# A trunk step on one core: which engine makes the low parts of the weights around the pooling groups, and three orders beside it

## The chip, the cores and the metric

The kernel runs on one core of one Trainium2 chip (trn2). The metric is the device time of one execution in microseconds. A core has TensorE (PE in the profile; its weight loads are PEld), VectorE (DVE), ScalarE (ACT), GpSimd (POOL) and SyncE (SP), which work side by side and wait for each other by semaphores, and 16 DMA engines that carry the transfers which SP, ACT and GpSimd issue.

## The reference

One layer of a hybrid trunk over 288 columns: 256 positions of a new sequence and 8 x 4 new tokens of running ones (with 30 old convolution inputs and 15 old pooling inputs each). Cut to what matters:

```python
h = rmsnorm(x, norm1_g)
proj = h @ w_in + b_in                     # 2048 -> 3072: a | gate | z, 1024 each
u = a * sigmoid(gate)
c = silu(layernorm(depthwise_causal_conv(u, 31 taps, conv_b), ln_g, ln_b))
d = mean of z over the last w positions - z          # four groups of 256 columns, w = 2, 4, 8, 16
p = d @ pool_w[g] * pool_scale                       # 256 x 256 for each group
x = x + concat([c, p]) @ w_out                       # 2048 -> 2048
f = relu(rmsnorm(x, norm2_g) @ w_ff1) ** 2           # 2048 -> 8192
x = x + f @ w_ff2                                    # 8192 -> 2048
y = rmsnorm(x, norm_f)
```

It also returns the last 30 columns of u and the last 15 of z.

## The kernel before

**Products in parts.** Each float32 operand is held as a high part, rounded to the matmul's format (`F32R`), and a low part, the rest. For a 128x128 block of weights and 288 columns there are three matmuls: high weight by high column, low weight by high column, high weight by low column. `gemm` writes them for two blocks k, k+1 as six in a row: the two of `whi`, the two of `wlo`, then `whi` again by the columns' low parts.

**The weights' way in.** The weights come as 512 KB tiles `wr` (128 partitions, four blocks of k, 256 columns, six buffers) by loads that SP issues in the order of use. ACT copies each into its high part `whi` (L260). The low part `wlo` is made in one of three ways, by a letter of the table `WAYS`, which names a few letters for each stage of the program and repeats them (`split_part`): G, two GpSimd subtractions of 128x512 (L268); V, one DVE subtraction of 128x1024 (L265); D, ACT writes minus the high part (L262) and a DMA on GpSimd's queue adds the weights from HBM onto it (L263), called an adding transfer here. `whi` and `wlo` have five buffers each, so ACT starts on a tile when PE is done with the tile five before.

I number the weight tiles in the order of use; PE has 24 matmuls on each of 512 KB. The stages are those of `SEQUENCE`: c0 and c1 (tiles 1 to 8), c2 (9 to 12), c3 (13 to 16), c4 (17 to 20), p3 (21 to 24), c5 (25 to 28), p2 (29 to 32), P3 (33, a half tile), c6 (34 to 37), p1 (38 to 41), P2 (42), p0 (43 to 46), P1 (47), c7 (48 to 51), P0 (52). A c is the projection of one 128-column piece of a and its gate, a p that of the 256 columns of z of a pooling group, a P the product of a group with its `pool_w`. Then come the lower half of w_out, by the pool columns `mixp` (stage names w0 to w7; buffers `dx` in the trace), its upper half by the convolution's columns `mixc` (`mx` in the trace), and the MLP.

**Beside the projections.** After a c, `conv_pair` makes u (DVE L432, L436, ACT's sigmoid), and then 30 taps by DVE on the 256 columns (L448), and for the tokens one GpSimd multiplication of all 31 windows into `prd` (L451) that DVE sums (L453). The taps stand under `later()`, so DVE takes them when nothing else of it is ready. `sum_c` is the running sum of the conv columns, by GpSimd (L456). After a p, `pool_group` adds neighbours on GpSimd, w doubling (L479), corrects the first columns (L483), and forms d: DVE the 256 columns (L484), GpSimd the 32 newest (a scaling L486, in place, and a subtraction L487). ACT and DVE split d (L489, L490).

**What sets the order.** A scheduler orders each engine's instructions by the priority of where they are written, with `later()` as an offset and `tc.issue_after` as a tie. Within some gemms the table `TURN` reorders the first 48 matmuls by a pattern of classes. PSUM banks (`ac`) have two pairs; a product starts when DVE has emptied the pair (L470, L432, in w_out the addition to x, L579).

The change touches `load`, `split_part`, `gemm`, `weight_groups`, `conv_pair`, `pool_group` and the lines of the main function that call them.

Of the kernel before, what the change touches and what calls it, by code (L numbers as in the profile page):

```python
# [86 lines left out]
def trunk_kernel(ctx: ExitStack, tc: tile.TileContext, io):  # L87
# [163 lines left out]

    turns = {}

    def split_part(raw, src, hi, lo, way):

        nc.scalar.copy(hi, raw)  # L260
        if way == "D":
            nc.scalar.activation(lo, f32(hi), AF.Copy, scale=-1.0)  # L262
            nc.gpsimd.dma_start(lo, src, accum_op=ALU.add)  # L263
        elif way == "V":
            nc.vector.tensor_tensor(lo, raw, f32(hi), op=ALU.subtract)  # L265
        else:
            for j in range(0, raw.shape[1], 2):
                nc.gpsimd.tensor_tensor(lo[:, j : j + 2, :], raw[:, j : j + 2, :], f32(hi[:, j : j + 2, :]), op=ALU.subtract)  # L268

# [25 lines left out]

    def gemm(banks, rhs, m_outer=False, between={}, classes="", by_part=False, gets=None, pairs=None):

# [129 lines left out]
    def conv_pair(i, banks):  # L427
# [9 lines left out]
        if i % 2 == 0:  # L437
            cs.append(actp.tile([P, 2, T], F32, name=nm("c"), tag="c", bufs=4))
        c = cs[i // 2][:, i % 2, :]
        with later():  # L440
# [10 lines left out]
            nc.gpsimd.tensor_tensor(prd[:, :, :, 0:CW], windows(us, CW), cwv[:, None, None, :].to_broadcast([P, NB, NS, CW]), op=ALU.mult)  # L451
# [12 lines left out]
    def pool_group(g):  # L464
# [19 lines left out]
        nc.vector.scalar_tensor_tensor(out=d[:, :, 0:SEQ], in0=s[:, :, PH:ZO], scalar=1.0 / w, in1=z[:, :, PH:ZO], op0=ALU.mult, op1=ALU.subtract)  # L484
# [1 line left out]
        nc.gpsimd.tensor_scalar(news[0], news[0], 1.0 / w, None, op0=ALU.mult)  # L486
        nc.gpsimd.tensor_tensor(d[:, :, SEQ:T].rearrange("p m (b t) -> p m b t", t=NS), news[0], news[1], op=ALU.subtract)  # L487
        dh, dl = act2("dx", tag="p", bufs=4)
# [50 lines left out]
    gemm(each(bks[0]) + each(bks[1]), proj, gets=[lambda k, m: both_gets[m // 2][0](k, m % 2)], between={(0, 2): lambda: pool_products(0)}, classes="." * 36 + TURN, pairs=early + [(6, m) for m in range(4)])  # L539
    chain.clear()  # L540
# [241 lines left out]
```

## Time and profile before

| | |
|---|---|
| median of 3 runs | 1081.81 us (1081.7 to 1082.16) |
| the profiled execution's own time | 1082.43 us |
| its span, first to last instruction | 1080.6 us |
| granted TensorE clock, mean | 0.998 |
| PE busy | 1069.2 us, 99% of the span, 8176 matmuls |
| DVE, ACT, POOL busy | 633.7, 479.0, 175.9 us |
| adding transfers (L263) | 7 of 512 KB |

Times are in microseconds from the span's start. A timeline row gives a start, a length, the engine, the line, and what it writes and reads; neighbours of one kind are put together (x6), and brackets hold the idle time ahead and what ended it. A row of the chain of waits gives a start, a length and a count of instructions that follow one another on the path that ended last. A row of stretches gives, for a window, its length and each engine's busy time with its count, then the granted clock, the DMA engines' mean busy share and what they moved in GB/s.

### The profile page before, as it was taken

The page shows a single profiled execution, that of the slowest core. Times are in us where ns is not written, and L with a number is a line of the kernel's source. Part 1 is how long each engine was busy: PE and PEld are TensorE (multiplying, and loading weights), DVE is VectorE, ACT ScalarE, POOL GpSimd, SP SyncE. Part 2 cuts the span into 40 slices and gives each one's busy share as a digit, 9 for nine tenths or more (in the row PEclk, how much of TensorE's full clock was granted, in tenths as well). Part 3 has the DMA queues.
Part 4 walks back from the last instruction along what each step waited for, and adds up shares of the span by engine and source line. Part 5 has one row for each costly group of instructions (what it writes and reads, how often), then busy time and mean ns, then how long its engine had stood idle before and what let it go on. Part 6 is the DMA issues. An engine that isn't in the chain of part 4 may idle for free.

```text
span 1080.6 us, 19528 instructions
## 1 busy us (share of the span) xinstructions
PE 1069.2 (99%) x8176; PEld 1067.9 (99%) x8176; DVE 633.7 (59%) x810; ACT 479.0 (44%) x588; POOL 175.9 (16%) x182
## 2 busy tenths in 40 slices
PE   9999999999999999999999999999999999999996
PEld 8999999999999999999999999999999999999996
DVE  7899999788654544444554444555544445554553
ACT  8654445665544433334443333444433334444441
POOL 0878979512000000000000000000000000000001
PEclk9999999999999999999999999999999999999999
DMA  9896478555555555555555555555555555555522
GB/s 326 288 263 182 145 187 247 177 171 173 162 173 166 169 175 163 170 173 165 170 174 164 170 170 167 171 173 162 173 168 167 173 171 164 173 166 170 172 79 88
DMA packets 58296, 190.71 MB, mean 176 GB/s; under 512 B 6240, under 2 KB 11232, under 8 KB 58208
## 3 DMA queue, kind: packets, MB, share of 16 engines
q1 hardware_dynamic: 56336, 184.35, 54.3%
q0 software_dynamic: 1008, 3.67, 1.9%
q8 instruction: 64, 1.05, 0.4%
q10 hardware_dynamic: 864, 1.44, 0.4%
q14 instruction: 24, 0.20, 0.0%
HBM read 185.16 MB, written 4.28 MB: 175 GB/s over the span
## 4 chain that ended last, share of the span: by engine, by line
PE 75%; issue 21%; ACT 2%; POOL 1%; DMA 1%; SPq 0%; POOLq 0%; DVE 0%
PE ac L291 74%; POOL wlo L268 1%; DMA wr<-in_w 1%; ACT whi L349 1%; PE pp L291 1%; DMA wlo<-in_w 1%; ACT hx L354 0%; ACT z_all L405 0%; POOL prd L451 0%; POOL xT L718 0%; ACT whi L260 0%; SPq L191 0%; POOLq L768 0%; DVE xT L691 0%; ACT whi L356 0%
## 5 line engine op out<-in xcount | busy, mean ns | idle before, releaser
L260 ACT CAST whi<-wr 128x1024 fp32r<-128x1024 f32 (+1 forms) x332 | 346.5, 1044 | 551.3 <-PE ac L291 536.7
L265 DVE TENSOR_TENSOR wlo<-wr,whi 128x1024 fp32r<-128x1024 f32 x288 | 353.5, 1227 | 348.1 <-ACT whi L260 348.1
L291 PE MATMUL ac<-ax,whi 128*128 128x288 f32 x2048 | 351.0, 292 | 0.0
L291 PE MATMUL ac<-fx,whi 128*128 128x288 f32 x2048 | 350.2, 292 | 0.0
L291 PEld LDWEIGHTS ac<-ax,whi 128*128 128x128 f32 x2048 | 296.0, 187 | 0.0
L291 PEld LDWEIGHTS ac<-fx,whi 128*128 128x128 f32 x2048 | 295.6, 187 | 0.0
L291 PE MATMUL ac<-ax,wlo 128*128 128x288 f32 x1024 | 217.3, 292 | 0.0
L291 PE MATMUL ac<-fx,wlo 128*128 128x288 f32 x1024 | 216.4, 292 | 0.0
L291 PEld LDWEIGHTS ac<-ax,wlo 128*128 128x128 f32 x1024 | 162.5, 187 | 0.0
L291 PEld LDWEIGHTS ac<-fx,wlo 128*128 128x128 f32 x1024 | 162.2, 187 | 0.0
L291 PE MATMUL ac<-hx,whi 128*128 128x288 f32 x768 | 131.9, 296 | 1.4 <-DVE hx L352 1.4
L718 POOL TENSOR_TENSOR xT<-xT,rf 128x288 f32<-128x288 f32 x4 | 3.1, 795 | 799.9 <-ACT rf L722 799.9
L291 PEld LDWEIGHTS ac<-hx,whi 128*128 128x128 f32 x768 | 112.6, 190 | 1.8 <-ACT hx L354 1.7
L268 POOL TENSOR_TENSOR wlo<-wr,whi 128x512 fp32r<-128x512 f32 x74 | 102.4, 1433 | 17.1 <-ACT whi L260 16.0
L448 DVE SCALAR_TENSOR_TENSOR pc<-u_all,vec,pc 128x256 f32<-128x256 f32 x232 | 99.3, 479 | 1.9 <-ACT pc L445 0.7
L291 PE MATMUL ac<-hx,wlo 128*128 128x288 f32 x384 | 80.4, 295 | 0.2 <-DMA wlo<-in_w 0.2
L291 PEld LDWEIGHTS ac<-hx,wlo 128*128 128x128 f32 x384 | 61.1, 189 | 0.4 <-DMA wlo<-in_w 0.4
L291 PE MATMUL ac<-dx,whi 128*128 128x288 f32 x256 | 46.8, 295 | 0.0
L291 PE MATMUL ac<-mx,whi 128*128 128x288 f32 x256 | 44.9, 293 | 0.0
L660 DVE SCALAR_TENSOR_TENSOR t<-ac,r 128x576 f32<-128x576 f32 x32 | 24.2, 757 | 25.4 <-PE ac L291 25.3
L291 PEld LDWEIGHTS ac<-dx,whi 128*128 128x128 f32 x256 | 38.4, 188 | 0.2
L291 PEld LDWEIGHTS ac<-mx,whi 128*128 128x128 f32 x256 | 37.5, 188 | 0.2 <-DVE xT L579 0.2
(129 smaller groups left out, 529.6 us busy)
## 6 DMA issues: line engine op xcount, KB each, us to landing
wr<-in_w SPq DMA_DIRECT2D x335, 512.0 KB, 3.8
wlo<-in_w POOLq DMA_DIRECT2D x7, 512.0 KB, 7.8
xT<-in_xT SPq DMA_DIRECT2D x8, 288.0 KB, 7.7
wr<-in_w SPq DMA_DIRECT2D x5, 256.0 KB, 3.9
out_u_out<-u_all SPq DMA_DIRECT2D x1, 1208.0 KB, 9.6
u_all<-in_hist_c SPq DMA_DIRECT2D x8, 136.0 KB, 5.3
out_z_out<-z_all SPq DMA_DIRECT2D x1, 668.0 KB, 9.2
z_all<-in_hist_p SPq DMA_DIRECT2D x4, 152.0 KB, 6.6
```

The costliest lines, as they stand in the source:

```text
L260: nc.scalar.copy(hi, raw)
L265: nc.vector.tensor_tensor(lo, raw, f32(hi), op=ALU.subtract)
L268: nc.gpsimd.tensor_tensor(lo[:, j : j + 2, :], raw[:, j : j + 2, :], f32(hi[:, j : j + 2, :]), op=ALU.subtract)
L291: last = nc.tensor.matmul(*args, **kw)
L349: nc.scalar.copy(hi[:, blocks[0]], raw[:, blocks[0]])
L448: nc.vector.scalar_tensor_tensor(out=dst, in0=up[:, w : w + SEQ], scalar=cwv[:, w : w + 1], in1=pc, op0=ALU.mult, op1=ALU.add)
L660: nc.vector.scalar_tensor_tensor(out=t, in0=bk[:, :, :T], scalar=0.0, in1=both(rows2[0]), op0=ALU.max, op1=ALU.mult)
L718: eng.tensor_tensor(xk, xk, r[:, None, :].to_broadcast([P, n, T]), op=ALU.mult)
```

## The change

It does six things.

1. `WAYS`: c4 turns from GDGD to GGGD (tile 18: G for D), p3 keeps GDDG under the general letter p, p2 turns from GVVG to GDDG (tiles 30 and 31: D for V), p1 to GVDG (tile 40), p0 to GDVG (tile 44), and w0 from VV to GV. Four low parts of pooling groups go from DVE to adding transfers, one of c4 goes from a transfer to GpSimd, and one of w0 from DVE to GpSimd: ten transfers for seven.
2. The multiplication `prd` is tied behind an adding transfer (first ones) or behind the newest columns of a pooling group (i over 4), and the taps of c2 and c3 are written one stage later.
3. `pool_group` writes GpSimd's part of d (scaling and newest columns) ahead of DVE's part.
4. GpSimd's subtractions of later tiles are tied behind a group's newest columns (`pooled`).
5. The halves of the tiles w0 to w7 are loaded and used in exchanged order (`load((1, 0))`, `^ 4`), the first 24 matmuls of the first w_out product put the columns' high parts ahead of the low parts, and the pool products P1 and P0 begin earlier inside the products around them.
6. In the first product over `mixc` the pairs of k and column block are taken in another order (`mixed`).

```diff
-WAYS = {... "c4": "GDGD", "p3": "GDDG", "c5": "GDGD", "c": "GGGV", "p": "GVVG", "w0": "VV", ...}
+WAYS = {... "c4": "GGGD", "c5": "GDGD", "c": "GGGV", "p0": "GDVG", "p1": "GVDG", "p": "GDDG", "w0": "GV", ...}
-    def load():
+    def load(order=(0, 1)):
-        for h in range(2):
+        for h in order:
-    turns = {}
+    turns, added, newest, pooled = {}, [], {}, []
         if way == "D":
             nc.scalar.activation(lo, f32(hi), AF.Copy, scale=-1.0)
-            nc.gpsimd.dma_start(lo, src, accum_op=ALU.add)
+            added.append(nc.gpsimd.dma_start(lo, src, accum_op=ALU.add))
...
-                nc.gpsimd.tensor_tensor(lo[:, j : j + 2, :], raw[:, j : j + 2, :], ...)
+                with tc.issue_after(pooled[-1].ins) if pooled else nullcontext():
+                    nc.gpsimd.tensor_tensor(lo[:, j : j + 2, :], raw[:, j : j + 2, :], ...)
...
+        todo[:late] = sorted(todo[:late], key=lambda p: p[2])          # in gemm, late=0 by default
...
-            get = split(load(), f"w{j}")
-            yield [lambda k, m, get=get: get(korder[k], m)]
+            get = split(load((1, 0)), f"w{j}")
+            yield [lambda k, m, get=get: get(korder[k] ^ 4, m)]
...
+        while waiting:                                                  # in conv_pair
+            taps(*waiting.pop())
+        if i in (2, 3):
+            waiting.append((i, up, us))
+        else:
+            taps(i, up, us)
+    def taps(i, up, us):
...
-            nc.gpsimd.tensor_tensor(prd[:, :, :, 0:CW], windows(us, CW), ...)
+            with tc.issue_after((newest[{5: 3, 6: 2, 7: 0}[i]] if i > 4 else added[max(0, min(2, i - 1))]).ins):
+                nc.gpsimd.tensor_tensor(prd[:, :, :, 0:CW], windows(us, CW), ...)
...
-        nc.vector.scalar_tensor_tensor(out=d[:, :, 0:SEQ], in0=s[:, :, PH:ZO], ...)
         news = [...]
         nc.gpsimd.tensor_scalar(news[0], news[0], 1.0 / w, None, op0=ALU.mult)
-        nc.gpsimd.tensor_tensor(d[:, :, SEQ:T]..., news[0], news[1], op=ALU.subtract)
+        last = nc.gpsimd.tensor_tensor(d[:, :, SEQ:T]..., news[0], news[1], op=ALU.subtract)
+        newest[g] = last
+        nc.vector.scalar_tensor_tensor(out=d[:, :, 0:SEQ], in0=s[:, :, PH:ZO], ...)
...
+        if i == 7:
+            pooled.append(newest[1])
-   ... between={12: lambda: pool_products(1)}
+   ... between={8: lambda: pool_products(1)}
         else:
+            pooled.append(newest[i])
             pool_products(i)
+    pooled.append(newest[0])
...
+    mixed = [(k, m) for k in range(0, KT // 2, 2) for m in range(4)]
+    mixed.sort(key=lambda km: (km[0] // 4, km[1] // 2) if km[0] < 4 else (1, 0))
-    gemm(... between={(0, 2): lambda: pool_products(0)}, classes="." * 36 + TURN, pairs=early + [(6, m) for m in range(4)])
+    gemm(... late=24, between={4: lambda: pool_products(0)}, classes="." * 24 + TURN, pairs=early + [(6, m) for m in range(4)])
...
-    gemm(each(bks[0]) + each(bks[1]), mixc, gets=[...])
+    gemm(each(bks[0]) + each(bks[1]), mixc, gets=[...], pairs=mixed)
```

The scheduler's result on GpSimd at the start of c3: the low part of tile 13 (`wlo_604`), the adding transfer of tile 14 (`wlo_609`), the multiplications of c0 and c1 and the low part of tile 15 (`wlo_618`). Before:

```order
L268 TENSOR_TENSOR wlo_604<-wr_599,whi_603 128x512 x2
L451 TENSOR_TENSOR prd_667<-u_all,vec 128x32x31
L451 TENSOR_TENSOR prd_708<-u_all,vec 128x32x31
L263 DMA wlo_609<-in_w 128x1024
L268 TENSOR_TENSOR wlo_618<-wr_613,whi_617 128x512 x2
```

and now:

```order
L269 TENSOR_TENSOR wlo_604<-wr_599,whi_603 128x512 x2
L263 DMA wlo_609<-in_w 128x1024
L463 TENSOR_TENSOR prd_667<-u_all,vec 128x32x31
L463 TENSOR_TENSOR prd_708<-u_all,vec 128x32x31
L269 TENSOR_TENSOR wlo_618<-wr_613,whi_617 128x512 x2
```

The transfer is issued ahead of the two multiplications. GpSimd again, from the sums of p1 to p0: the low part of tile 41 (`wlo_1703` before, `wlo_1706` now), that of tile 43 (`wlo_1894`, `wlo_1897`), tile 46 (`wlo_1911`, `wlo_1915`), and now the transfers of tile 40 (`wlo_1701`) and tile 44 (`wlo_1902`). Before:

```order
L479 TENSOR_TENSOR s_1528<-s_1525 128x416 x2
L268 TENSOR_TENSOR wlo_1703<-wr_1696,whi_1702 128x512 x2
L483 TENSOR_TENSOR s_1528<-s_1528,rcnt 128x2x7
L486 TENSOR_SCALAR s_1528<-s_1528 128x2x8x4
L487 TENSOR_TENSOR d_1531<-s_1528,z_all 128x2x32
L451 TENSOR_TENSOR prd_1746<-u_all,vec 128x32x31
L268 TENSOR_TENSOR wlo_1894<-wr_1889,whi_1893 128x512 x2
L268 TENSOR_TENSOR wlo_1911<-wr_1904,whi_1910 128x512 x2
```

and now:

```order
L263 DMA wlo_1701<-in_w 128x1024
L491 TENSOR_TENSOR s_1530<-s_1527 128x416 x2
L269 TENSOR_TENSOR wlo_1706<-wr_1698,whi_1705 128x512 x2
L495 TENSOR_TENSOR s_1530<-s_1530,rcnt 128x2x7
L497 TENSOR_SCALAR s_1530<-s_1530 128x2x8x4
L498 TENSOR_TENSOR d_1533<-s_1530,z_all 128x2x32
L463 TENSOR_TENSOR prd_1749<-u_all,vec 128x32x31
L269 TENSOR_TENSOR wlo_1897<-wr_1892,whi_1896 128x512 x2
L468 TENSOR_TENSOR sum_c<-sum_c,c_1019 128x288
L263 DMA wlo_1902<-in_w 128x1024
L269 TENSOR_TENSOR wlo_1915<-wr_1908,whi_1914 128x512 x2
```

The two transfers stand among the sums, and the transfer of tile 44 stands behind the subtraction of tile 43 and an addition to `sum_c`. PE at the start of the products over `mixc`: `ac22` is the pair of banks of column blocks 0 and 1, `ac23` that of 2 and 3. Before:

```order
728 L291 MATMUL ac22_2841<-mx1_2816,whi69_2741 128x288 x4
729 L291 MATMUL ac22_2841<-mx1_2816,wlo69_2742 128x288 x2
730 L291 MATMUL ac22_2841<-mx1_2816,whi69_2741 128x288 x2
731 L291 MATMUL ac23_2842<-mx1_2816,whi71_2803 128x288 x2
732 L291 MATMUL ac23_2842<-mx1_2816,wlo71_2804 128x288 x2
733 L291 MATMUL ac23_2842<-mx1_2816,whi71_2803 128x288 x4
```

and now:

```order
722 L292 MATMUL ac22_2846<-mx1_2821,whi69_2746 128x288 x4
723 L292 MATMUL ac22_2846<-mx1_2821,wlo69_2747 128x288 x2
724 L292 MATMUL ac22_2846<-mx1_2821,whi69_2746 128x288 x2
725 L292 MATMUL ac22_2846<-mx2_2828,whi69_2746 128x288 x2
726 L292 MATMUL ac22_2846<-mx2_2828,wlo69_2747 128x288 x2
727 L292 MATMUL ac22_2846<-mx2_2828,whi69_2746 128x288 x4
728 L292 MATMUL ac22_2846<-mx2_2828,wlo69_2747 128x288 x2
729 L292 MATMUL ac22_2846<-mx2_2828,whi69_2746 128x288 x2
730 L292 MATMUL ac23_2847<-mx1_2821,whi71_2808 128x288 x2
```

The first pair of banks gets 24 matmuls ahead of the second, where it got 12: its two blocks of the second columns (`mx2`) stand in between.

More of the change, by code (lines that the diff above doesn't have):

```diff
@@ L70 @@
 TURN = "110100" * 4 + "01" * 6 + "1100" * 3
-WAYS = {"c2": "GVGV", "c3": "GDGG", "c4": "GDGD", "p3": "GDDG", "c5": "GDGD", "c": "GGGV", "p": "GVVG", "w0": "VV", "w": "GG", "ff": "VV"}
+WAYS = {"c2": "GVGV", "c3": "GDGG", "c4": "GGGD", "c5": "GDGD", "c": "GGGV", "p0": "GDVG", "p1": "GVDG", "p": "GDDG", "w0": "GV", "w": "GG", "ff": "VV"}
 VEC = (("norm1_g", 16), ("b_in", 24), ("conv_b", 8), ("ln_g", 8), ("ln_b", 8), ("pool_scale", 8), ("norm2_g", 16), ("norm_f", 16))
@@ L267, in split_part @@
             for j in range(0, raw.shape[1], 2):
-                nc.gpsimd.tensor_tensor(lo[:, j : j + 2, :], raw[:, j : j + 2, :], f32(hi[:, j : j + 2, :]), op=ALU.subtract)
+                with tc.issue_after(pooled[-1].ins) if pooled else nullcontext():
+                    nc.gpsimd.tensor_tensor(lo[:, j : j + 2, :], raw[:, j : j + 2, :], f32(hi[:, j : j + 2, :]), op=ALU.subtract)
     def spl():
@@ L294, in mm, with gemm @@
         return last
-    def gemm(banks, rhs, m_outer=False, between={}, classes="", by_part=False, gets=None, pairs=None):
+    def gemm(banks, rhs, m_outer=False, between={}, classes="", by_part=False, gets=None, pairs=None, late=0):
         n = len(rhs)
@@ L412, in trunk_kernel @@
     rb = row("rb")
-    cs, pcs = [], []
+    cs, pcs, waiting = [], [], []
     sum_c = tmpp.tile([P, 2, T], F32, name="sum_c", tag="ag2", bufs=2)
@@ L450, in conv_pair @@
             nc.scalar.activation(prd[:, :, :, CW], ones[:, 0 : NB * NS].rearrange("p (b t) -> p b t", t=NS), AF.Identity, bias=v("conv_b", i), scale=0.0)
-            nc.gpsimd.tensor_tensor(prd[:, :, :, 0:CW], windows(us, CW), cwv[:, None, None, :].to_broadcast([P, NB, NS, CW]), op=ALU.mult)
+            with tc.issue_after((newest[{5: 3, 6: 2, 7: 0}[i]] if i > 4 else added[max(0, min(2, i - 1))]).ins):
+                nc.gpsimd.tensor_tensor(prd[:, :, :, 0:CW], windows(us, CW), cwv[:, None, None, :].to_broadcast([P, NB, NS, CW]), op=ALU.mult)
             cso = c[:, SEQ:T]
@@ L483, in pool_group @@
         nc.gpsimd.tensor_tensor(first_sums, first_sums, rcnt[:, None, w - 2 : 2 * w - 3].to_broadcast([P, 2, w - 1]), op=ALU.mult)
-        nc.vector.scalar_tensor_tensor(out=d[:, :, 0:SEQ], in0=s[:, :, PH:ZO], scalar=1.0 / w, in1=z[:, :, PH:ZO], op0=ALU.mult, op1=ALU.subtract)
         news = [x[:, :, ZO:ZL].rearrange("p m (b t) -> p m b t", t=ZS)[:, :, :, PH:] for x in (s, z)]
         nc.gpsimd.tensor_scalar(news[0], news[0], 1.0 / w, None, op0=ALU.mult)
-        nc.gpsimd.tensor_tensor(d[:, :, SEQ:T].rearrange("p m (b t) -> p m b t", t=NS), news[0], news[1], op=ALU.subtract)
+        last = nc.gpsimd.tensor_tensor(d[:, :, SEQ:T].rearrange("p m (b t) -> p m b t", t=NS), news[0], news[1], op=ALU.subtract)
+        newest[g] = last
+        nc.vector.scalar_tensor_tensor(out=d[:, :, 0:SEQ], in0=s[:, :, PH:ZO], scalar=1.0 / w, in1=z[:, :, PH:ZO], op0=ALU.mult, op1=ALU.subtract)
         dh, dl = act2("dx", tag="p", bufs=4)
@@ L527, in trunk_kernel @@
             continue
+        if i == 7:
+            pooled.append(newest[1])
         if kind == "c":
-            conv_pair(i, conv_products(i, classes=TURN if i == 5 else "", **(dict(gets=ahead(1), between={12: lambda: pool_products(1)}) if i == 7 else {})))
+            conv_pair(i, conv_products(i, classes=TURN if i == 5 else "", **(dict(gets=ahead(1), between={8: lambda: pool_products(1)}) if i == 7 else {})))
         elif kind == "p":
@@ L538, in trunk_kernel @@
     early.sort(key=lambda km: km[1] // 2)
-    gemm(each(bks[0]) + each(bks[1]), proj, gets=[lambda k, m: both_gets[m // 2][0](k, m % 2)], between={(0, 2): lambda: pool_products(0)}, classes="." * 36 + TURN, pairs=early + [(6, m) for m in range(4)])
+    mixed = [(k, m) for k in range(0, KT // 2, 2) for m in range(4)]
+    mixed.sort(key=lambda km: (km[0] // 4, km[1] // 2) if km[0] < 4 else (1, 0))
+    gemm(each(bks[0]) + each(bks[1]), proj, gets=[lambda k, m: both_gets[m // 2][0](k, m % 2)], late=24, between={4: lambda: pool_products(0)}, classes="." * 24 + TURN, pairs=early + [(6, m) for m in range(4)])
     chain.clear()
@@ L598, in trunk_kernel @@
     two_gets = [ahead(0) for _ in range(2)]
-    gemm(each(bks[0]) + each(bks[1]), mixc, gets=[lambda k, m: two_gets[m // 2][0](k, m % 2)])
+    gemm(each(bks[0]) + each(bks[1]), mixc, gets=[lambda k, m: two_gets[m // 2][0](k, m % 2)], pairs=mixed)
     chain.clear()
```

## The prediction

> **What bounds the kernel now.** First the page's busy times and the list of what PE waited for. The columns of the last three rows are total, times, longest.
>
> ```profile
> PE 1069.2 (99%) x8176; PEld 1067.9 (99%) x8176; DVE 633.7 (59%) x810; ACT 479.0 (44%) x588; POOL 175.9 (16%) x182
> PE ac L291 <- DVE hx L352: 1.4, 1, 1.4
> PE warm L214 <- DVE cst L231: 1.0, 1, 1.0
> PE ac L291 <- DMA wlo<-in_w: 0.2, 1, 0.2
> ```
>
> PE is the bound, with 2.6 us of waits, of which 2.4 are at the start, which the change leaves alone. So there is no stage in which an engine could give back much: what is to be had is the 0.2, and what PE loses without waiting. For that I read the chain of waits, whose pieces have a count each.
>
> ```profile
> 44.41 5.97 DMA wlo<-in_w
> ...
> 50.42 60.24 PE ac L291 x454
> ...
> 112.22 24.96 PE ac L291 x192
> ...
> 171.50 26.61 PE ac L291 x204
> ...
> 208.53 74.07 PE ac L291 x564
> ```
>
> PE's step is 24.96 / 192 = 0.130 us. At this pace 454 matmuls take 59.02 us, and the piece that begins with the DMA takes 60.24: 1.22 too many. The piece of 204, which holds a `TURN` order, is 0.09 over, the last one 0.75. All other pieces between 45 and 283 us are at 0.130. The timeline shows both places. PE at the first, with the start of tile 14 and the low part of tile 23 far behind it, and that of tile 44:
>
> ```profile
> 49.55 0.68 PE L291 MATMUL ac<-hx,whi 128*128 128x288 f32 x4
> 50.42 0.54 PE L291 MATMUL ac<-hx,wlo 128*128 128x288 f32 x2 [0.20 <-DMA wlo<-in_w]
> ...
> 78.52 0.43 PE L291 MATMUL ac<-hx,wlo 128*128 128x288 f32 x2
> ...
> 79.32 0.43 PE L291 MATMUL ac<-hx,wlo 128*128 128x288 f32 x2
> ...
> 141.96 0.42 PE L291 MATMUL ac<-hx,wlo 128*128 128x288 f32 x2
> ```
>
> Four steps after 49.55 the low part of tile 14 should begin, at 50.07; it begins at 50.42, 0.35 late. Afterwards six matmuls take 79.32 - 78.52 = 0.80 instead of 0.78: a stall is followed by a slower step, which lasts (the later pieces are at 0.130 again) until the `TURN` order of c5. GpSimd and ACT ahead of that stall:
>
> ```profile
> 38.90 1.30 POOL L268 TENSOR_TENSOR wlo<-wr,whi 128x512 fp32r<-128x512 f32 x1
> 40.16 4.33 POOL L451 TENSOR_TENSOR prd<-u_all,vec 128x992 f32<-128x992 f32 x2
> 44.41 1.01 POOL L263 DMA_DIRECT2D wlo<-in_w  x1
> 39.26 1.06 ACT L262 ACTIVATE wlo<-whi 128x1024 fp32r<-128x1024 f32 x1
> ```
>
> ACT had minus the high part ready at 40.32, and GpSimd issued the transfer at 44.41, behind two multiplications of 4.33 us together. The second place is the first product over `mixc`; PE, then DVE:
>
> ```profile
> 218.41 0.68 PE L291 MATMUL ac<-mx,whi 128*128 128x288 f32 x4
> 219.19 0.90 PE L291 MATMUL ac<-mx,whi 128*128 128x288 f32 x4
> 218.09 0.75 DVE L590 TENSOR_TENSOR mx<-n,mx 128x576 fp32r<-128x576 f32 x1
> 218.75 0.74 DVE L579 TENSOR_TENSOR xT<-xT,ac 128x576 f32<-128x576 f32 x1
> ```
>
> Four matmuls take 0.90 for 0.68: the first matmul of column block 2 waits until the addition to x at 218.75 has emptied its banks, at 219.49.
>
> **The change, part by part.** *The transfer of tile 14 ahead of the multiplications.* It can be issued at 40.3 and lands, in 5.97 us as now, at 46.3, 3.7 before it is needed. That takes away 0.35 of stall, and of the 1.22 what the slow step made: 0.13 may be a record not counted at the piece's border, which leaves 1.1, and 0.09 is a `TURN`'s own price and stays. 0.35 + 1.1 - 0.1 = 1.35; I take 1.3. The two multiplications, and behind them the low parts of tiles 15 and 16, come 1 us later for the issue; the low part of tile 15 then ends near 49 and PE needs it at 53.7 - 0.4.
>
> *The mixed pairs.* Block 2 is first written 12 matmuls later, 24 steps after the product's start at 217.89 (four steps ahead of the row at 218.41): 221.0, 1.5 behind the end of the addition. The second pair of `mx` is then needed at 217.89 + 1.56 = 219.45, and the subtraction at 218.09 ends at 218.84, with its low part used last. So 0.22 goes. Of the last piece's 0.75, 0.22 is this stall, 0.09 a `TURN`, 0.13 a possible record at the border; about 0.3 is left for the slow step behind it, and I take 0.25, since a single matmul pair of the norm also stands at that piece's start. Together 0.45.
>
> *Four subtractions from DVE to transfers.* For GpSimd, these rows (its subtraction pairs undisturbed and beside DVE's, its waits for DVE, DVE's subtraction, and the next addition to `sum_c`):
>
> ```profile
> 68.90 0.87 POOL L263 DMA_DIRECT2D wlo<-in_w  x1 [2.04 <-ACT wlo L262]
> 70.84 2.54 POOL L268 TENSOR_TENSOR wlo<-wr,whi 128x512 fp32r<-128x512 f32 x2 [1.06 <-ACT whi L260]
> ...
> 102.56 0.39 POOL L486 TENSOR_SCALAR s<-s 128x64 f32<-128x64 f32 x1 [0.81 <-DVE d L484]
> ...
> 128.83 0.38 POOL L486 TENSOR_SCALAR s<-s 128x64 f32<-128x64 f32 x1 [0.81 <-DVE d L484]
> ...
> 129.60 2.21 POOL L451 TENSOR_TENSOR prd<-u_all,vec 128x992 f32<-128x992 f32 x1
> 131.76 4.13 POOL L268 TENSOR_TENSOR wlo<-wr,whi 128x512 fp32r<-128x512 f32 x2
> ...
> 142.59 0.81 POOL L456 TENSOR_TENSOR sum_c<-sum_c,c 128x288 f32<-128x288 f32 x1
> 133.53 1.21 DVE L265 TENSOR_TENSOR wlo<-wr,whi 128x1024 fp32r<-128x1024 f32 x1
> 131.02 1.05 ACT L260 CAST whi<-wr 128x1024 fp32r<-128x1024 f32 x1 [0.68 <-PE ac L291]
> ```
>
> A pair takes 2.54 alone and 4.13 with a DVE subtraction inside it. Each of the four costs GpSimd 0.88 for the issue, and gives back about 1.0 (between nothing and 4.13 - 2.54 = 1.59; other DVE work shares that difference). ACT gets 1.06 each, with waits of 0.68 in its row above; DVE loses five subtractions of about 1.21, 6 us. None of these engines bounds PE, so by itself this costs and gives nothing. What counts is when the transfers land, for which I have the range of the seven and the DMA engines' share in stretches (second number from the right):
>
> ```profile
> DMA to landing us min/median/max: 6.0/7.8/10.2
> 44.41:50.40 5.99, 5.82 (x45) 5.59 (x43) 5.63 (x14) 3.58 (x7) 5.99 (x7) 1.00 0.67 150
> 68.90:78.80 9.90, 9.90 (x77) 9.90 (x76) 8.95 (x23) 5.34 (x8) 8.15 (x7) 1.00 0.98 252
> 104.00:120.00 16.00, 16.00 (x126) 16.00 (x125) 15.92 (x30) 9.58 (x15) 16.00 (x13) 1.00 0.47 137
> 133.00:142.00 9.00, 9.00 (x72) 9.00 (x71) 9.00 (x20) 4.64 (x9) 6.50 (x6) 1.00 0.51 174
> ```
>
> A transfer that is issued as soon as ACT has written minus the high part has 79.32 - 68.90 = 10.4 us until PE needs it. Tiles 30, 31 and 40 stand among short sums and lose about 1 us of that: 9.3 to land, against 7.8. They are free of cost. The narrow one is tile 44, behind a row of GpSimd without a gap (16.00 of 16.00). The multiplication of c6 ends at 131.81 before. Two waits of 0.81 go, three issues of 0.88 come, three DVE subtractions give back 1.0 each: 129.8; if the whole row comes as much earlier as PE (1.3), 128.5. Then one pair, 2.54 (to 3.5), and 0.81: issue between 131.8 and 134.1, and by ACT not before 131.02 + 1.05 + 1.06 - 1.3 = 131.8. PE needs the tile at 141.96 - 1.3 = 140.7. So there are 6.6 to 8.9 us, middle 7.9. The ends for the landing are 6.0 and 10.2; at the share of 0.51 there the nearest row is the one of 0.67, with 6.0, so I take 6.0 to 6.5 and no cost.
>
> The Trainium skill (SBUF — State Buffer, Who interferes with whom) states that a DVE instruction with two SBUF inputs contends with a GpSimd instruction that reads SBUF, and that the loser blocks for the whole instruction. By this rule each of the three subtractions would give back its full 1.21, and the transfer of tile 44 would go out 0.6 earlier; the 4.13 beside 2.54 agrees in kind.
>
> *One transfer fewer in c4, for a GpSimd pair.* GpSimd gets 2.54 - 0.88 = 1.7 near 55 us; the pairs there end some 9 us ahead of PE and the waits of 2.04 and 1.06 in the rows at 68.90 and 70.84 take it up. Tile 23's transfer has 10.4 us and takes 9.9: 0.5 to spare. A multiplication stands ahead of it now, 2.2 us, which eats about what the earlier row saved; one transfer fewer ahead of it makes the landing shorter. I take nothing, with 0.3 late as the bad end.
>
> *Newest columns first.* It takes 1.6 us of waiting from GpSimd before tile 44 (counted above) and makes DVE's part of d 0.38 + 0.35 later. Its reader is a pool product that starts 9 us later or more. *P1 and P0 earlier, w0's halves, the high parts first, w0's first V to G*: the same matmuls in another order, at most 24 steps (3.1 us) apart; the products' columns are ready by more than that, and GpSimd has idle time behind 144 us. Nothing; as an unknown order can cost or spare a slow step, 0.1 to 0.3 either way.
>
> Sum: -1.3 - 0.45 = -1.75. The profiled execution took 1082.43, so 1080.7; the median of the runs is 0.62 below it, so 1080.1, a gain of 0.16%. A measurement of this kernel can tell about 0.2%, 2.16 us, from no change.
>
> **The rivals.** *A: the gain stays, and tile 44 stalls PE.* For it: 7.8 us of landing are the median of the seven, as much as there is. Against: the low share at that place. Late by 0.5 it costs 0.5, a first double step (0.54 for 0.42, 0.1) and the slow step from 141 to the next `TURN` near 171, 30 us x 0.02 / 0.78 = 0.8: 1.4, so 1081.5; late by 1.2, 1082.2.
>
> *B, slower: landings as in the busiest stretch, 10.2, for all four.* Tile 30 would be 0.9 late, tile 40 0.9, tile 44 2.3 to 3.6, 31 carried by the stall before; 0.1 each; and the slow step would run from 101 to 171, 1.8. That is 6.2 to 7.5, less 1.75: 1086.3 to 1087.6, in the middle 1086.9. It decides (over 0.2% slower, so 3.9 us lost) from landings of 9.5 us on. For it: 9.9 at a share of 0.98, and the added transfers raise the share. Against: 0.47 and 0.51 where three of the four are.
>
> The Trainium skill (DMA: Bandwidth & Descriptors, Issuing engines are not separate DMA queues) states that transfers of all issuing engines run on the same 16 DMA engines and interleave, which speaks against this change. The landing of 6.0 at a share of 0.67 and 9.9 at 0.98 bears it out; by the rule alone the time would be B's.
>
> *C, faster by over 0.2%.* All that PE loses over 0.130 between 45 and 283 us is 0.35 + 1.22 + 0.09 + 0.75 = 2.4. If the new orders also spare what I left, the time is 1079.5. Against: two `TURN` orders stay.
>
> *D: no gain.* The transfer of tile 14 lands as late as now, since the weight loads crowd it, or the slow step has another cause than the stall. Then 0.45 at most is left: 1081.4. Against: 3.7 us to spare.
>
> **How the numbers follow.** Forecast 0.58, A 0.20, C 0.13, B 0.05, D 0.04. The forecast's own range is 1079.8 to 1080.8; with A, C and D the range is 1079.5 to 1081.9, which leaves out B and A's far end. Faster by over 0.2% (below 1079.65) holds C and little of the forecast: 0.16. Slower (above 1083.97) is B: 0.05. The rest is the same: 0.79.
>
> **What would show it.** Right: the transfer of tile 14 is issued near 40.4, PE's list has no wait for a DMA, pieces of the chain between 50 and 110 are at 0.130 but for `TURN`, and four matmuls near 218 take 0.68 each time. Wrong: a new wait of PE for a DMA near 78 or 141, groups of six at 0.80 in the trace after it, or low parts that GpSimd makes late.

## The result, and the profile after

The changed kernel takes 1086.16 us in the median of five runs (1084.55 to 1087.9), the kernel before 1081.81 beside it: a ratio of 1.0035, 95% interval 1.0021 to 1.0048. It is slower by 4.35 us; the forecast was 1.75 faster. Its profiled execution took 1085.12 us (span 1083.3), 2.7 over that of before, so the lines below can account for 2.7 of the 4.35 us.

The busy times, and the one new line in the list of what PE waited for (total, times, longest):

```profile
PE 1068.7 (99%) x8176; PEld 1067.3 (99%) x8176; DVE 635.0 (59%) x805; ACT 481.6 (44%) x591; POOL 181.7 (17%) x189
PE ac L292 <- DMA wlo<-in_w: 2.9, 1, 2.9
```

DVE has five instructions fewer than before and 1.3 us more busy time. The chain of waits, where the pieces of the prediction stand again:

```profile
78.02 31.45 PE ac L292 x238
...
136.24 7.58 DMA wlo<-in_w
...
143.86 15.99 PE ac L292 x118
...
161.45 9.60 PE ac L292 x72
...
211.24 73.58 PE ac L292 x564
```

The piece that was 1.22 us too long before is gone: nothing stands at 50 us now. The last one is 0.49 shorter than before (74.07). In between there is a transfer of 7.58 us, and behind it PE runs at 9.60 / 72 = 0.1333 instead of 0.130 (the piece of 118 is at 0.1355, since it holds a double first step), up to the `TURN` order of the first w_out product. PE there, and GpSimd at the place of tile 14:

```profile
140.25 0.68 PE L292 MATMUL ac<-hx,whi 128*128 128x288 f32 x4
143.86 0.54 PE L292 MATMUL ac<-hx,wlo 128*128 128x288 f32 x2 [2.93 <-DMA wlo<-in_w]
40.50 1.06 POOL L263 DMA_DIRECT2D wlo<-in_w  x1 [0.74 <-POOL wlo L269]
```

The low part of tile 44 should begin at 140.77 and begins at 143.86: 3.09 late. Both gains of the prediction came (about 1.3 and 0.49). What was lost: 3.09; the double first step behind it, 0.11; about 0.7 by the slower step up to 172; and 0.35 in three smaller delays at 74 to 78 (tiles 22 and 23), with 0.2 by a slow step behind them. The losses less the gains are 2.7 us, which is what this execution lost. The rest of the 4.35 lies in executions without a trace and stays open.

### The profile page after: what moved, and what is told of

It reads as the page before. It is cut to its first block, busy times and chain, and to the rows that moved or that the text cites. A ratio compares the mean times of both kernels' runs of the same rounds, so it can differ in the third digit from the quotient of the medians.

```text
span 1083.3 us, 19540 instructions
## 1 busy us (share of the span) xinstructions
PE 1068.7 (99%) x8176; PEld 1067.3 (99%) x8176; DVE 635.0 (59%) x805; ACT 481.6 (44%) x591; POOL 181.7 (17%) x189
## 4 chain that ended last, share of the span: by engine, by line
PE 75%; issue 20%; POOL 2%; DMA 1%; DVE 0%; POOLq 0%; ACT 0%
PE ac L292 75%; POOL wlo L269 1%; DMA wlo<-in_w 1%; POOL s L491 0%; DMA wr<-in_w 0%; PE pp L292 0%; POOL xT L737 0%; POOL prd L463 0%; PE norm L292 0%; POOLq L787 0%; DVE xT L710 0%; ACT whi L351 0%; POOL s L495 0%; PE pmean L292 0%; DVE hx L354 0%
## 5 line engine op out<-in xcount | busy, mean ns | idle before, releaser
L265 DVE TENSOR_TENSOR wlo<-wr,whi 128x1024 fp32r<-128x1024 f32 (+1 forms) x283 | 350.8, 1239 | 347.3 <-ACT whi L260 347.3
L269 POOL TENSOR_TENSOR wlo<-wr,whi 128x512 fp32r<-128x512 f32 x78 | 107.8, 1451 | 18.9 <-ACT whi L260 14.4
```

## The experiments

The experiments ask three things: why tile 44's transfer goes out late, whether DVE is a bound beside PE, and whether the two gains come when they are alone. Each ratio is to the kernel before, run beside it on the same chip (median 1082.0 to 1082.2, and 1081.81 for the first row). The third column has the places where PE stood, in us from the start, with the time lost against a step of 0.130. The medians come from 5 to 12 executions each, the places from one. For e4 and e9 that one is the slowest of its runs (1090.88 and 1088.75), so their places say more than their medians do.

| run | median, us; ratio and interval | PE stood at: us |
|---|---|---|
| changed kernel | 1086.16; 1.0035 (1.0021 to 1.0048) | 78: 0.2, 141: 3.1 |
| e1 tile 44 by DVE | 1084.80; 1.0023 (1.0014 to 1.0032) | 77: 0.1, 171: 1.5 |
| e2 tile 43 by DVE | 1085.06; 1.0022 (1.0013 to 1.0031) | 75 and 78: 0.5, 142: 2.0 |
| e3 DVE's d first | 1091.06; 1.0080 (1.0067 to 1.0093) | 130: 1.1, 142: 5.8 |
| e3c three things | 1087.06; 1.0045 (1.0032 to 1.0058) | 100: 0.2, 137: 0.7, 143: 0.6, 174: 1.3, 183: 0.3 |
| e15 tile 43, no c6 multiplication | 1082.39; 1.0001 (0.9992 to 1.0009) | 140: 2.2 |
| e10 fewer taps | 1083.25; 1.0013 (1.0004 to 1.0021) | 78: 0.5, 171: 0.5, 176: 0.7, 180: 0.4 |
| e11 no added transfers | 1085.27; 1.0031 (1.0018 to 1.0043) | 166: 1.9, 171: 1.7, 181: 0.6 |
| e7 w_out order | 1084.22; 1.0022 (1.0013 to 1.0031) | 129: 1.0, 171: 1.1 |
| e8 TURN in c6 | 1084.91; 1.0028 (1.0018 to 1.0037) | 129: 0.1, 170: 1.4 |
| e13 pool_w by transfers | 1085.19; 1.0030 (1.0018 to 1.0041) | 136: 1.5, 169: 1.3 |
| e4 tie alone | 1086.57; 1.0048 (1.0035 to 1.0060) | 62: 3.3, 165 to 178: 2.4 |
| e9 tie, mixed pairs | 1085.22; 1.0029 (1.0020 to 1.0038) | 62: 2.8, 164 to 178: 2.4 |
| e12 tie, mixed, c4 | 1084.72; 1.0024 (1.0015 to 1.0033) | 68 to 78: 1.0, 160 to 174: 2.4 |
| e5 mixed alone | 1081.77; 0.9996 (0.9987 to 1.0004) | 50: 0.3 |
| e16 mixed, TURN in c4 | 1081.35; 0.9992 (0.9984 to 1.0001) | 50: 0.3 |

### Why tile 44's transfer goes out late

The rows of the changed kernel around it, GpSimd, then DVE, then ACT:

```profile
128.38 0.34 POOL L498 TENSOR_TENSOR d<-s,z_all 128x64 f32<-128x64 f32 x1
129.79 2.19 POOL L463 TENSOR_TENSOR prd<-u_all,vec 128x992 f32<-128x992 f32 x1 [1.07 <-DVE u_all L438]
131.93 3.60 POOL L269 TENSOR_TENSOR wlo<-wr,whi 128x512 fp32r<-128x512 f32 x2
135.49 0.81 POOL L468 TENSOR_TENSOR sum_c<-sum_c,c 128x288 f32<-128x288 f32 x1
136.24 0.89 POOL L263 DMA_DIRECT2D wlo<-in_w  x1
...
130.02 2.52 DVE L500 SCALAR_TENSOR_TENSOR d<-s,z_all 128x512 f32<-128x512 f32 x1
...
133.62 0.75 DVE L503 TENSOR_TENSOR dx<-d,dx 128x576 fp32r<-128x576 f32 x1
...
134.68 0.47 DVE L459 SCALAR_TENSOR_TENSOR c<-u_all,vec,pc 128x256 f32<-128x256 f32 x1
...
132.62 0.68 ACT L502 CAST dx<-d 128x576 fp32r<-128x576 f32 x1 [2.42 <-DVE d L500]
133.20 1.05 ACT L260 CAST whi<-wr 128x1024 fp32r<-128x1024 f32 x1
134.28 1.07 ACT L262 ACTIVATE wlo<-whi 128x1024 fp32r<-128x1024 f32 x1
```

What the transfer needs comes late from three engines. GpSimd ends tile 43's pair at 135.5, adds to `sum_c` and issues the transfer at 136.24. That addition needs DVE's last tap, done at 135.15. And ACT has minus the high part of tile 44 at 135.35: its copy of p2's columns (L502) stands ahead of tile 44's two instructions and waits 2.42 us for DVE's d, which takes 2.52 us for 0.69, since GpSimd's multiplication of c6 began 0.23 ahead of it. From here on the theory is that all three hold it. The rivals are that GpSimd's row alone holds it, which is the step of the prediction, and that the landing is what is long.

**e1**, tile 44 by DVE again:

```diff
-"p0": "GDVG"
+"p0": "GVVG"
```

> The changed kernel with tile 44's low part by DVE's subtraction again (p0 GVVG), nothing else undone. If the loss is the stall at tile 44 (3.09 us of gap and a slower step up to the TURN near 172, 1.1 us): no wait of PE for a DMA over 0.5 us, steps of 0.130 after 141, own time of the profiled execution about 1080.9, about 1081 in the median, which is 0.999 of before. Rival, that the added transfers as such crowd the DMA engines: another transfer (tiles 30, 31, 40 or 23) becomes late, 1083 or more.

The stall at 141 is gone, but the median falls by 1.4 us, not by 5. PE stood at 171 instead, waiting for DVE:

```profile
PE ac L292 <- DVE u_all L438: 1.4, 1, 1.4
172.69 0.37 PE L292 MATMUL ac<-dx,whi 128*128 128x288 f32 x1 [1.35 <-DVE u_all L438]
171.90 0.64 DVE L438 SCALAR_TENSOR_TENSOR u_all<-ac,vec,tg 128x256 f32<-128x256 f32 x2
by line: DVE pc L459 52.9%; DVE wlo L265 18.1%; DVE d L500 7.1%; issue 5.2%; DVE dx L503 4.5%; DVE c L465 3.1%; DVE dx L515 2.9%; DVE u_all L438 2.2%; DVE ac L434 2.1%; DVE c L459 1.1%; DVE tz L482 1.1%; DVEq L265 0.1%
```

The last line is the chain of waits from 97 to 172.6 us, by line: almost all of it is DVE's. It empties c7's banks 1.5 us too late for the second pair of banks of the first w_out product. In the changed kernel tile 44's stall had covered this, for PE came to that place later. PE also ran at 0.1333 from 99 to 171, 1.8 us in all, though it stood for no more than 0.02 at 99. So both halves of the expectation missed: no other transfer stalled it, and it didn't reach 1081.

**e2**, tile 43 by DVE, and **e15**, the same with c6's multiplication and sum left out:

```diff
-"p0": "GDVG"
+"p0": "VDVG"
...
+            if i != 6:      # e15 alone; else the token columns get the bias
                 prd = ...
```

> The changed kernel with tile 43's low part by DVE instead of GpSimd (p0 VDVG): GpSimd has neither that pair nor the addition to sum_c ahead of tile 44's transfer. Rival, the step of the prediction, that GpSimd's own row decides: the transfer goes out near 132.5 instead of 136.24, lands by 140.1, the stall of 3.1 us is gone and the time is about 1081. Theory, that ACT, GpSimd and DVE are late at once: ACT's minus high part stays at 135.3 behind its copy of p2's columns, the transfer goes out at 135.4, the stall is still over 2 us, the time 1085.

> The changed kernel with tile 43 by DVE, and c6's GpSimd multiplication with DVE's sum of it left out (the 32 token columns of one piece of the convolution are the bias alone). Theory, that this instruction of 2.19 us beside it makes DVE's d of p2 2.52 instead of 0.69 us and so holds ACT's copy of d, its high part of tile 44 and the minus high part behind it: d takes 0.7, minus the high part is ready by 133.6 instead of 135.99, the transfer goes out then instead of 136.28, and the stall at tile 44 falls from 2.0 to 0.5 us or less. Rival, that ACT or the pace of PE's buffers makes it late: the transfer goes out after 135.5, the stall stays near 2.

DVE's d, ACT's minus high part and the transfer, first of e2, then of e15, with their places in the two chains of waits and, last in each, the stretch of the transfer's own time:

```profile
130.65 2.52 DVE L500 SCALAR_TENSOR_TENSOR d<-s,z_all 128x512 f32<-128x512 f32 x1
134.92 1.07 ACT L262 ACTIVATE wlo<-whi 128x1024 fp32r<-128x1024 f32 x1
136.28 0.89 POOL L263 DMA_DIRECT2D wlo<-in_w  x1 [3.67 <-ACT wlo L262]
136.28 7.53 DMA wlo<-in_w
136.28:143.81 7.53, 5.71 (x43) 5.47 (x42) 7.53 (x16) 4.83 (x10) 6.01 (x6) 1.00 0.95 250
```

```profile
129.57 0.69 DVE L503 SCALAR_TENSOR_TENSOR d<-s,z_all 128x512 f32<-128x512 f32 x1
132.09 1.04 ACT L262 ACTIVATE wlo<-whi 128x1024 fp32r<-128x1024 f32 x1
133.44 0.89 POOL L263 DMA_DIRECT2D wlo<-in_w  x1 [5.16 <-ACT wlo L262]
133.44 9.05 DMA wlo<-in_w
133.44:142.49 9.05, 7.00 (x54) 6.77 (x53) 9.01 (x20) 5.77 (x11) 7.55 (x8) 1.00 0.87 234
```

In e2 GpSimd's row is empty, and GpSimd stands idle 3.67 us for ACT: its own row did not decide. The transfer goes out at 136.28, as late as in the changed kernel; the stall is shorter because PE was itself 1.06 us later there.

In e15 d takes 0.69, minus the high part is ready at 133.13 and the transfer goes out 2.84 earlier, at the time that the theory gave to 0.2 us. Of these 2.84, 1.83 are d's shorter time. The rest is not d's: this execution was ahead, with 0.4 at its start and fewer delays of PE at 75 to 130, so DVE came to d 1.08 earlier and PE to tile 44 1.55 earlier.

The expected stall of 0.5 did not come true: the transfer took 9.05 us, and PE stood 2.25. The share of the DMA engines does not tell the two landings apart, for it was 0.95 over e2's 7.53 us and 0.87 over these 9.05. SP's loads moved more beside it, 1.59 MB for 1.36 in e2. That is one execution, at 1083.74; e15's twelve runs go from 1080.04 to 1084.3, and their median is 2.7 below e2's (DVE has a sum of 1.21 us less to do there, too). So the issue is explained, and the landing is a second cause that I had sized too small.

**e3**, DVE's d written first again, and **e3c**, with tile 43 by DVE and an addition to `sum_c` left out besides:

```diff
+        nc.vector.scalar_tensor_tensor(out=d[:, :, 0:SEQ], ...)
         news = ...
         nc.gpsimd.tensor_scalar(news[0], ...)
         last = nc.gpsimd.tensor_tensor(d[:, :, SEQ:T]..., ...)
         newest[g] = last
-        nc.vector.scalar_tensor_tensor(out=d[:, :, 0:SEQ], ...)
```

> The changed kernel with DVE's part of d written ahead of GpSimd's newest columns again, as before. Theory: DVE's d of p2 takes 0.7 instead of 2.5 us, since GpSimd waits for it and starts its multiplication only afterwards; ACT's copy of d then stands near 130 and minus the high part of tile 44 is ready by 133.5 instead of 135.35, but GpSimd's row gets its wait of 0.8 back and still ends near 135.5, so the transfer goes out at about 135.5 and the stall is 2 to 3 us; 1084 to 1086. Rival, that the newest columns first alone make it late: the transfer goes out by 133.5 and the stall is under 1 us; 1081 to 1082.

> The changed kernel with three things ahead of tile 44's transfer taken away together: DVE's d first, tile 43's low part by DVE, and one addition to sum_c left out (the first column of c4 is missing in the mean of the layer norm, so the output differs). Theory: the transfer goes out at 132 to 133, lands at 138 to 140.5, PE does not wait, 1080.5 to 1081.5. Rival, that the landing is what is long here: it takes over 8 us even so, PE waits over 0.5 us, 1082 or more.

Both expectations fell. GpSimd and DVE of e3:

```profile
124.50 2.76 POOL L269 TENSOR_TENSOR wlo<-wr,whi 128x512 fp32r<-128x512 f32 x2
127.00 1.92 POOL L491 TENSOR_TENSOR s<-s 128x416 f32<-128x416 f32 x2
129.00 0.56 POOL L495 TENSOR_TENSOR s<-s,rcnt 128x14 f32<-128x14 f32 x1
133.21 0.38 POOL L498 TENSOR_SCALAR s<-s 128x64 f32<-128x64 f32 x1 [3.65 <-DVE d L496]
...
125.56 3.92 DVE L265 TENSOR_TENSOR wlo<-wr,whi 128x512 fp32r<-128x512 f32 x1
```

A DVE subtraction of a pool_w tile, 0.69 alone, took 3.92 while GpSimd ran one instruction behind another, and ended (129.48) with GpSimd's row (129.56). DVE's d came at 132.43, GpSimd waited 3.65 for it, and tile 44's transfer went out at 140.89, 4.65 later than in the changed kernel. In e3c the same instruction took 3.93 and the transfer went out at 137.51. So writing GpSimd's newest columns first was not the harm: without it the kernel is 5 us slower. The landing was not long in e3c, 5.94 us, so its rival fell as well.

### DVE as the second bound

**e10**, e1 with nine of DVE's taps left out:

```diff
-            for w in range(1, CW):
+            for w in range(4 if 3 < i < 7 else 1, CW):
```

> The kernel with tile 44 by DVE, and nine of DVE's taps left out (three each of c4, c5 and c6; their output columns differ), 9 x 0.39 = 3.5 us less for DVE ahead of c7's end, and nothing less for any other engine. Theory, that DVE is the second bound and empties c7's banks too late: the wait of PE for DVE near 171 (1.5 us) is gone, about -1.6 us against the run with tile 44 by DVE, 1083.2. Rival, that the order of the first w_out product or ACT makes that wait: it stays over 1 us, 1084.8.

The median is 1.55 lower, as expected, though the two intervals overlap. The wait at 171 falls from 1.5 to 0.5, not to nothing, and what is left of it goes through ACT, whose sigmoid stands between DVE's two steps there:

```profile
170.41 0.64 DVE L438 SCALAR_TENSOR_TENSOR u_all<-ac,vec,tg 128x256 f32<-128x256 f32 x2 [0.57 <-ACT tg L436]
```

PE then waits for DVE again, at 176 (0.7, for a low part of the pool columns) and at 180 (0.4, for an addition to x). In this execution (1084.11, the slower side of its runs) PE loses as much between 171 and 180 as in e1, 1.5 us. So DVE's taps do set the wait at 171, and taking them away moves the wait on more than it ends it.

**e11**, all four added transfers undone:

```diff
-"p0": "GDVG", "p1": "GVDG", "p": "GDDG"
+"p3": "GDDG", "p": "GVVG"
```

> The changed kernel with the four added transfers of p2, p1 and p0 undone (p3 GDDG, the others GVVG), the rest of the change kept. Theory: no stall near 78, 100, 130 and 141, but DVE has 3.7 us more work than with tile 44 alone undone and empties c7's banks later, so the wait near 171 grows from 1.5 to 3 us or more: 1084 to 1087. Rival, that the transfers as such are the loss: no wait of PE over 0.3 us, 1080 to 1081.5.

No transfer is late, and PE stands 1.9, 1.7 and 0.6 us for DVE between 166 and 181, which is the theory's side. **e7** gave the first w_out product its old order, **e8** added `TURN` to c6:

```diff
-gemm(... late=24, between={4: ...}, classes="." * 24 + TURN, ...)      # e7 and e8
+gemm(... between={(0, 2): ...}, classes="." * 36 + TURN, ...)
-classes=TURN if i == 5 else ""                                         # e8
+classes=TURN if i in (5, 6) else ""
```

> The kernel with tile 44 by DVE, and the first w_out product as before (P0 ahead of the second pair of banks, 36 matmuls ahead of TURN, no sorting of the first 24); its second pair of banks is then first written 48 matmuls behind c7 instead of 36, 6.2 us instead of 4.7. Theory, that DVE empties c7's banks about 6 us behind c7 and that tile 44's stall only hid this: the wait of 1.5 us near 171 goes, -1.6 us against the run with tile 44 by DVE, 1083.2. Rival, that DVE is late for another reason and the wait moves with it: no gain, 1084.8.

> The same kernel with TURN's order in c6 too; only PE's order changes. Theory, that a hiccup puts PE on a step of 0.1333 which a TURN order takes back to 0.130: the step is 0.130 from c6's middle (about 116) up to the next stall, where the run before has 0.1333 from 99 to 172, -1.3 us against it if it has such a stretch. Rival, that the slow step has another cause (GpSimd's or DMA's work beside it): 0.1333 goes on behind c6, no gain.

With 12 matmuls more for DVE, and a stall of PE of 1.0 at 129 besides, e7's wait at 171 is still 1.1. So the rival held: DVE is late for more than the order. e8 is inconclusive, since neither e7's profile nor its own had a slow stretch ahead of c6 to end. **e13** made the low parts of the four pool_w tiles by transfers too:

```diff
-split_part(raw[:, 0:2, :], None, ..., "V")
+split_part(raw[:, 0:2, :], io["w"][0][:, 2 * g : 2 * g + 2, :], ..., "D")
```

> The kernel with tile 44 by DVE, and the low parts of the four pool_w tiles by adding transfers of 256 KB instead of DVE's 128x512 subtractions. These four took 6.7 us of DVE between 84 and 171 where undisturbed ones take 0.69 each. Theory, that DVE is the second bound: DVE is 4 to 6 us ahead near c7, the wait near 171 is gone, 1083.2; GpSimd pays 0.88 for each issue. Rival: GpSimd's row or a late transfer makes a new wait of the same size, 1084.8 or more.

The wait at 171 went, and two came: P2 for DVE's low part of d, 1.3, and P0 for one of the new transfers, 1.1. So the rival held.

### The two terms alone

**e4** put only the tie into the kernel before, **e9** the mixed pairs as well, **e12** c4's GGGD besides:

```diff
+            with tc.issue_after(added[0].ins) if i < 2 else nullcontext():
                 nc.gpsimd.tensor_tensor(prd[:, :, :, 0:CW], ...)
```

> The kernel before with one part of the change: the two multiplications of c0 and c1 stand behind the adding transfer of tile 14. The term of the prediction: the transfer goes out near 40.4, the stall of 0.35 us at 50 and the slow step behind it go, -1.3 us. Rival, that a tie at this place moves other things: GpSimd's and DVE's later instructions are placed anew by the scheduler, another transfer (tile 20 to 28) or DVE's subtraction comes late, and the gain is under 0.5 us or a loss.

> The kernel of the run with the tie alone, and the mixed pairs at the start of the products over mixc. Prediction's second term: four matmuls near 218 take 0.68 instead of 0.90 and no slow step follows, -0.45 us against the tie alone, together -1.75 us, about 0.9984 of before. Rival: the wait moves to the next banks or to the second columns of mixc, no gain from it.

> The kernel before with the tie of the multiplications, the mixed pairs and c4's GGGD, so that tile 18's low part is made by GpSimd and not by the transfer that came 3 us late in the run with the tie alone. Theory: no stall near 62 and none at 50; PE then comes 1.3 us earlier to c7 than DVE, and the waits for DVE and ACT near 164 to 178 (2.9 us in all in the run with the tie and the mixed pairs) stay at 1.5 to 3 us: 1081.5 to 1083.5. Rival, the prediction's sum: 1080.1.

The stall at 50 went in all three, but none of them became faster. In e4 the rival held: tile 18's transfer, one stage on, came 3.3 us late (a piece of its chain of waits), and PE went on at half clock (granted 0.50), which the stretch behind shows:

```profile
55.73 9.72 DMA wlo<-in_w
65.50:71.20 5.70, 5.70 (x24) 5.70 (x25) 2.98 (x4) 0.03 (x1) 0.26 (x1) 0.50 1.05 287
```

It was issued 0.87 later than before and took 9.72 us, and PE wanted it 1.2 earlier. In e9 the mixed pairs did what was expected (e4 has a delay of 0.10 at 227 with a slow step behind it, e9 has none), but not the sum, for tile 18 is late there too. e12 takes that transfer away, as the change does, and its theory's places came: no stall at 50 or 62, and waits for DVE and ACT of 2.4 us between 160 and 174, the same as in the other two between 164 and 178. The prediction's sum, its rival, did not come. Its time is 1.2 above the range that I gave even so; 1.0 us of new delays at 68 to 78 were not expected.

**e5** put only the mixed pairs into the kernel before, **e16** `TURN` in c4 as well:

```diff
+gemm(... mixc, ..., pairs=mixed)                  # e5 and e16
-classes=TURN if i == 5 else ""                    # e16
+classes=TURN if i in (4, 5) else ""
```

> The kernel before with the mixed pairs alone, which stand behind DVE's tight stretch. The prediction's second term: the 0.22 us near 219 and the slow step behind it up to 230 go, -0.45 us, 1081.6 where before is 1082.04 (0.9996). Rival: the wait moves, no gain.

> The same with TURN's order in c4 too; no other engine's order changes. Theory of the slow step: the step goes back from 0.1333 to 0.130 near 66 instead of 88, -0.5 us, of which DVE's lead of 0.5 us at c7's banks keeps most: 1081.1. Rival, that DVE takes it all back near 171: a wait for DVE there, 1081.6.

Two pieces of e16's chain of waits:

```profile
49.85 59.69 PE ac L291 x454
...
207.41 73.58 PE ac L291 x564
```

The pieces were 60.24 and 74.07 before: 0.55 and 0.49 gained, and no wait for DVE near 171. e5 has the 0.49 alone. In time both fit what was expected (-0.36 and -0.78), but both intervals still reach 1. e16 is the fastest version that I have, by a difference that its runs alone don't prove.

## Why the prediction was wrong, point by point

- **Tile 14's transfer first**: right, issue at 40.50 (40.4 forecast), no wait at 50, about 1.3 us, as forecast. **Mixed pairs**: right, 0.49 for 0.45, shown again in e5 and e16.
- **Issue of tile 44's transfer**: this is the step that failed, 136.24 for 131.8 to 134.1. I summed GpSimd's row (its multiplication was to end at 129.8, and ended at 131.98) and took ACT's row at 131.02 as a floor that moves with PE. It does not: ahead of it in ACT's order stands the copy of d, which waits for DVE, and DVE's d took 2.52 us for 0.69. This is shown by e2 (GpSimd idle for 3.67 us, issue at 136.28) and by e15 (d at 0.69 again, and 1.83 of the 2.84 earlier).
- **Its landing**: 7.58 for 6.0 to 6.5. I took the share of a stretch of before, 0.51, in which no adding transfer ran; over the transfer's own 7.58 us it was 0.86. The share is a poor guide besides (0.95 in e2 for 7.53). What SP's loads moved during the transfer orders the landings better: 0.37 MB and 5.97 us for tile 14 before, and for tile 44 0.51 and 5.94 in e3c, 1.13 and 7.58 in the changed kernel, 1.36 and 7.53 in e2, 1.59 and 9.05 in e15. A longer landing also gives the loads more time, so this does not show which is the cause. Together, issue and landing make 3.09 where rival A had 0.5 to 1.2: the right place, 2.6 to 6 times too small. That 1086.16 lies beside B's 1086.3 is luck: B had all four transfers land as late as 10.2, and the ten land in 8.0 in the median, 7.8 before.
- **Tile 23's transfer, "nothing, with 0.3 late as the bad end"**: it was 0.17 late and tile 22's 0.07; with the slow step behind them this cost 0.6.
- **"DVE loses five subtractions of about 1.21, 6 us"** and **1.0 given back to GpSimd for each**: wrong in what became of them. Stretches of 84 to 171 us, before and after (third busy time is DVE's):

```profile
84.00:171.00 87.00, 87.00 (x671) 87.00 (x670) 84.20 (x171) 42.42 (x64) 74.84 (x66) 1.00 0.61 179
84.00:171.00 87.00, 84.07 (x641) 83.84 (x640) 85.39 (x170) 44.35 (x65) 76.81 (x71) 1.00 0.72 193
```

  DVE is busier after than before. Against the shortest time that each kind takes, its instructions lost about 5 us there before and about 10 after (summed over the trace). Most of the difference is in the pool_w tiles' subtractions (0.6 and 3.6) and in d (0.7 and 2.2), which the new order puts beside GpSimd's row more often. The sentence on DVE and GpSimd that I cited from the Trainium skill (SBUF — State Buffer, Who interferes with whom) agrees with this; I had used it for what GpSimd gets back, and not for what DVE pays.
- **Newest columns first, a reader "9 us later or more"**: wrong as a cover. DVE's low part of p2's d ended at 134.37 and P2 began at 135.83; and the reader that mattered was ACT's copy, 0.1 us behind d. That the step itself did harm is not shown; e3 speaks against it.
- **What bounds the kernel**: incomplete. PE was the bound, but DVE emptied c7's banks at 171.00 (row below, of before), and PE wrote to them at 171.50. What PE gains ahead of c7 beyond these 0.5 us or so is given back there, unless DVE gains as much:

```profile
170.37 0.63 DVE L436 SCALAR_TENSOR_TENSOR u_all<-ac,vec,tg 128x256 f32<-128x256 f32 x2
```

  e1's chain and e11 show it, e10 in part; the waits of e4, e9 and e12 agree, and so does e16, which gained 0.55 and has no wait. So even without the stall the 1.75 would not have been kept.
- **The orders of w_out and of P1 and P0 "nothing"**: the second pair of banks is wanted 36 matmuls behind c7 for 48 before, 1.6 us less room for DVE. In e7, which gives it back, the wait is 0.4 shorter than in e1; their intervals overlap, so what the order cost is not shown.

Open are why a wait of 0.02 us starts the step of 0.1333, and how much of the spread of the changed kernel's runs (3.4 us) is the landing. e15's spread of 4.3 us suggests that it is much of it, but no run isolates it.

## What to carry to other kernels

Where one engine is 99% busy, look for the engine that is only just ahead of it, at the places where they meet (a bank to be emptied): a gain is worth little more than that lead, 0.5 us here, unless the other engine gains too. Before an instruction's time is moved to another engine, follow what each in-order queue has standing ahead of it; a copy that waits for a third engine holds everything behind it. And take a saved VectorE instruction at its price only if the GpSimd work beside it stays where it was.

## What the runs showed of the hardware

- GpSimd can hold off a DVE instruction with two inputs in SBUF for longer than one of its own instructions: 3.92 us for a subtraction of 0.69 in e3, through the rest of a run of five. DVE's taps (one input in SBUF, one in PSUM) stayed at 0.46 to 0.49 in every run. The Trainium skill (SBUF — State Buffer, Who interferes with whom) has the loser block for the whole instruction; here it lost several in a row.
- Stalls of PE of very different sizes (0.02 us in e1, 3.1 in the changed kernel) were followed by a step of 0.1333 for 0.130, until a `TURN` order. The exception is e4: behind its 3.3 us and the half clock the step was 0.130 at once, from 71.4 on.
- After stalls of 2.8 (e9), 3.3 (e4) and 5.8 us (e3) PE went on at half clock (steps of 0.240, granted clock 0.50); after 3.1 in the changed kernel it did not. The clock was at half for 3.41 us in e9 and for 6.83, twice that, in e4 and e3. The stretches of 3.41 us around the fall, of e9, and those that share the stall in the changed kernel (its clock record has changes at 9.51 and 1077.88, 313 such steps apart, from which I counted):

```profile
62.50:65.91 3.41, 0.73 (x6) 0.56 (x5) 3.41 (x11) 2.10 (x2) 3.38 (x3) 1.00 1.04 268
65.91:69.32 3.41, 3.41 (x16) 3.41 (x16) 2.93 (x4) 0.00 (x0) 0.14 (x1) 0.50 1.04 344
69.32:72.73 3.41, 3.41 (x28) 3.41 (x27) 0.00 (x0) 2.60 (x4) 0.19 (x1) 1.00 0.94 227
...
139.21:142.62 3.41, 1.72 (x14) 1.49 (x12) 3.41 (x7) 0.95 (x3) 2.27 (x2) 1.00 0.89 192
142.62:146.04 3.42, 2.18 (x16) 2.18 (x17) 3.42 (x9) 2.71 (x6) 3.42 (x4) 1.00 0.71 253
```

  In the stretch ahead of the fall PE (first busy time) was busy for 0.73 us in e9, 1.11 in e4 and 1.22 in e3. In the changed kernel the stall fell on both sides of a border, and on each side PE was busy for 1.7 us or more. The Trainium skill (TensorE: Matmul & The Clock Gate, Part 1: The HAM clock gate (the "warmup" mystery)) has the slow clock after an idle window of about 3.4 us, free-running. These four runs agree with the window's length, but in none of the three that fell was PE idle for the whole window ahead of the fall.
